# Summing a tile over its partitions: by VectorE and a small matmul, or by TensorE from the whole tile

## The chip, the cores and the metric

The kernel runs on one core of one Trainium2 chip. A core has TensorE (PE in the profile, its weight loads PEld), VectorE (DVE), ScalarE (ACT), GpSimd (POOL) and SyncE (SP, which here only starts DMAs). The metric is device time in microseconds (us); the kernel before took 1765.57 us, the median of 3 runs from 1759.98 to 1765.77.

## The reference, cut to what matters

A token matrix of 256 x 1024 passes through a GLA layer, a grouped mixture of experts (moe0), an mLSTM layer, a second mixture (moe1), and then two transformer layers (l0, l1), each of attention and an MLP. The change touches one small thing in the last two: six rows that scale and shift the activations, made from a vector c that does not depend on the tokens.

```python
c_act = jax.nn.silu(c)                          # 1 x 1024
for l in range(DEPTH):                          # DEPTH = 2
    ada = c_act @ w_ada[l] + b_ada[l]           # (1 x 1024) @ (1024 x 6144)
    sh1, sc1, gt1, sh2, sc2, gt2 = jnp.split(ada, 6, axis=-1)
    h = rms(x, g_mix[l]) * (1.0 + sc1) + sh1    # ahead of attention
    ...
    x = x + gt1 * (mixed @ w_out[l])            # attention's output projection
    h2 = rms(x, g_mlp[l]) * (1.0 + sc2) + sh2   # ahead of the MLP
    x = x + gt2 * (square(relu(h2 @ w_ff1[l])) @ w_ff2[l])
```

## The kernel before, in words

All matrix work is done in float32 precision by three matmuls of a high and a low part: each weight chunk (128 x 1024) is copied to `hi` by ScalarE or VectorE, and `lo = w - hi` is made by VectorE or GpSimd. Dense products accumulate in PSUM tiles `mm` or `acc`. The instructions of every engine stand in the order in which the Python program emits them; the program keeps a clock of its own (class `Clock`, costs in `Timed.cost`) and lets it choose between two engines (`Either`, names `VG`, `VG2`, `AV`), and between emitting a side task's next step or not. Side tasks are generators that `B.tick()` advances between groups of matmuls. The profile puts nearly every instruction on line 175, where the recording wrapper calls the engine, so rows are told apart by tile names.

The modulation `c_act @ w_ada` is such a side task: `ada_cols` (line 1854). A product of a vector with a matrix would use one column of TensorE, so the other engines do it. There are 24 blocks of 512 output columns, numbered n = 0 to 23 (twelve per layer, j = n % 12), each in four quarters q = 0 to 3; a quarter is a DMA of 512 KB into `ada_w` (two buffers, on SP's queue in order with all weight loads), a scaled copy by ScalarE into an `ada_t` tile (128 x 512), a multiply-add of the other half by VectorE, and for q > 0 an add into the block's sum `acc`. There are 96 quarters. A quarter's buffer comes free after its multiply-add, and only then the load of the quarter two further on is issued (line 1904). The three `ada_t` tiles are shared out by `ada_used` (line 1893). In moe1 two free ones also take expert weights (`ada_room`).

After q = 3, `acc` holds 128 partial sums per column, one per partition, and these have to be added over the partitions. Lines 1924 to 1929 do most of it on VectorE: a transposition in blocks of 32 x 32, then a sum over each block's rows, which leaves `part` (128 x 16). Then `reduce` (line 1932), a hook that waits in the list `hooks`, makes four matmuls of 32 output rows against a constant `c_fold` (lines 2441 and 2468). In the trace each float32 matmul is two records, so a reduction shows 8 MATMUL and 8 LDWEIGHTS. Its result is copied to `raw`, the bias is added into `adac`, and for some j the scale and shift columns `mod` are made.

Where a reduction's matmuls stand on TensorE is decided by whoever takes a hook out of the list: the start or the middle of a dense product (lines 580 to 586, 601, 628 to 634), the output projection (line 670), an idle moment of draining (line 512), or `ada_need` (line 1957), which is called where the program cannot go on without a block: it advances side tasks until the block is done, and emits no other matmul meanwhile. In layer l0 that is block 9, needed by the normalization ahead of the MLP (line 2318). Side tasks are also paced: `calm` (line 1950) holds a step back while its engine is behind, and line 1890 holds q = 1 while more than one reduction waits.

Of the kernel before, what the change touches and what calls it, by code (L numbers as in the profile page):

```python
# [26 lines left out]
F32 = mybir.dt.float32  # L27
# [4 lines left out]
OP = mybir.AluOpType  # L32
AX = mybir.AxisListType

P = 128
# [192 lines left out]
def tile_model(ctx: ExitStack, tc: tile.TileContext, I, out, stages=None, h_in=None):  # L228
    nc = tc.nc
    clock = Clock()  # L230
    PE, V, A, G = [Timed(clock, e, n) for e, n in
                   ((nc.tensor, "PE"), (nc.vector, "V"), (nc.scalar, "A"), (nc.gpsimd, "G"))]
# [8 lines left out]
    const = ctx.enter_context(tc.tile_pool(name="const", bufs=1))  # L241
# [163 lines left out]
    def kp_view(W, r0, rows, n0, n):  # L405
        return W[r0:r0 + rows, n0:n0 + n].rearrange("(k p) n -> p k n", p=P)
# [164 lines left out]
    hooks = Hooks()  # L571
# [205 lines left out]
    def gla():  # L777
# [23 lines left out]
        def load_ng(nb):  # L801
            ngs[nb] = bcast_row(ph, I["gla_norm_g"][:, nb * 512:(nb + 1) * 512], "row", 512)
        load_ng(0)
        small_loads()
        glr = early.tile([17, T], F32, name="glr")
        S.pump()
# [177 lines left out]
        if "l0" in stages:  # L984
            B.push(ada_cols(), side=True)
# [859 lines left out]
    ada_T, ada_used = [], {}  # L1845
# [8 lines left out]
    def ada_cols():  # L1854

        todo = [(l, j, q) for l in range(2) if f"l{l}" in stages for j in range(12) for q in range(4)]
        ws = {}

        def load(i):
            if i < len(todo) and i not in ws and not ada_stop:  # L1860
                l, j, q = todo[i]
                ada_open[0] += 1
                w = clock.slot("ada_w", 2, ada.tile([P, 2, 512], F32, name="ada_w", tag="ada_w", bufs=2))
                SP.dma_start(w, kp_view(I["w_ada_2"][l], q * 256, 256, j * 512, 512))
                ws[i] = w

        first = {g: next((i for i, (u, _) in enumerate(S.chunks) if S.units[u][3] == g), 0) for g in ("l0", "l1")}
        NB = (4, 10, 16, 22, 24)
        CB = [first["l0"] - 30, first["l0"] + 36, first["l1"] - 24, first["l1"] + 40, first["l1"] + 90]

        def start(x):
            i = max(j for j in range(4) if x >= NB[j])
            return CB[i] + (CB[i + 1] - CB[i]) * (x - NB[i]) / (NB[i + 1] - NB[i])

        load(0)
        load(1)
        yield 14
        ada_T.extend(ada.tile([P, 512], F32, name="ada_t", tag=tag, bufs=n) for tag, n in
              (("ada_acc", 1), ("ada_t", 2), ("ada_t", 2)))
        acc = None  # L1880
        for i, (l, j, q) in enumerate(todo):
            n = i // 4
            ada_at[0] = lambda: (load(i), load(i + 1))
            while i not in ws:
                load(i)
                load(i + 1)
                yield 6 if i in ws else 1
            while n >= 4 and S.chunk_at < start(n + q / 4):
                yield
            while q == 1 and len(hooks.fs) > 1:  # L1890
                yield
            w = ws[i]
            ada_used[n, q] = (n + (0, 2, 1, 2)[q]) % 3
            t = ada_T[ada_used[n, q]]
            if n >= 4:
                yield from calm("A", w)
            A.activation(t, w[:, 0], AF.Copy, scale=ccol[:, 2 * q:2 * q + 1])
            if n >= 4:
                yield from calm("V", t)
            else:  # L1900
                yield
            V.scalar_tensor_tensor(t, w[:, 1], ccol[:, 2 * q + 1:2 * q + 2], t, op0=OP.mult, op1=OP.add)
            ada_open[0] -= 1
            load(i + 2)
            if q:
                if n >= 4:
                    yield from calm("G", t)
                else:
                    yield 1
                VG2.tensor_tensor(acc, acc, t, op=OP.add)  # L1910
                if q < 3:
                    del ada_used[n, q]
            else:
                acc = t
                if n < 4:
                    yield 1
            if q < 3:
                yield
                continue
            if n >= 4:  # L1920
                yield from calm("V", acc)
            else:
                yield
            part = small.tile([P, 4, 4], F32, name="part", bufs=3)
            V.transpose(t, acc)
            if n >= 4:
                yield from calm("V")
            V.tensor_reduce(part.rearrange("p k r -> p (k r)"), t.rearrange("p (b i) -> p b i", i=32), axis=AX.X,
                            op=OP.add)
            del ada_used[n, 0], ada_used[n, 3]  # L1930

            def reduce(ps, l=l, j=j, part=part):
                for r in range(4):
                    PE.matmul(ps[32 * r:32 * r + 32, 0:4], c_fold, part[:, :, r], start=True, stop=True,
                              skip_group_check=True)
                k = slice(4 * j, 4 * j + 4)
                raw = small.tile([P, 4], F32, name="raw", bufs=2)
                AV.copy(raw, ps[:, 0:4])
                VG2.tensor_tensor(adac[:, l, k], raw, bada[:, l, k], op=OP.add)
                if j % 6 == 3:  # L1940

                    w = j // 6
                    V.tensor_copy(mod[:, l, w, 1], adac[:, l, 24 * w:24 * w + 8])
                    V.scalar_tensor_tensor(mod[:, l, w, 0], adac[:, l, 24 * w + 8:24 * w + 16], 1.0,
                                           gcol[:, l * 2 + w], op0=OP.add, op1=OP.mult)
                ada_done.add((l, j))
            hooks.append(reduce, part)
            yield

    def calm(e, *aps):  # L1950
        for _ in range(10):
            t = max([clock.t[e]] + [clock.last(clock.span(a), False, e) for a in aps])
            if t <= clock.t["PE"] + 0.9:
                return
            yield
# [474 lines left out]
    c_ident = ident  # L2430
# [7 lines left out]
                SP.dma_start(h[a * 64:a * 64 + 64, mt], rows[2 * mt + a])  # L2438
    n_kept = _OFFS[4][0]
    cst = const.tile([P, n_kept - P], F32, name="cst")  # L2440
    c_fold = const.tile([P, 32], F32, name="fold")
    c_ones, c_iota, c_earl = [cst[:, o - P:o - P + n] for o, n in _OFFS[1:4]]
    mhalf = const.tile([P, 16], F32, name="mhalf")
    G.memset(mhalf, -0.5)
# [20 lines left out]

    def small_loads():
        ld = SP.dma_start
        V.tensor_reduce(c_fold, c_ident.rearrange("p (b m) -> p m b", m=32), axis=AX.X, op=OP.add)
        ld(cst, I["cst"][:, P:n_kept])
        ld(rwg[:, 0], I["router_w"].rearrange("(k p) n -> p k n", p=P))  # L2470
        for a, n in enumerate(("ln_g", "ln_b")):
            ld(lnpk[:, a], I[n][:, 0].rearrange("l (p k) -> p l k", k=8))
        ld(gatew, I["mlstm_w_in"][0][:, 4096:4104].rearrange("(k p) n -> p k n", p=P))
        for a in range(2):
            ld(bg[32 * a:32 * a + 4], I["mlstm_b_gates"][0, 4 * a:4 * a + 4].unsqueeze(1))
        ld(crow[0:64], I["mlstm_conv_w"][0].rearrange("j (f p) -> (j f) p", p=P))
        ld(crow[64:80], I["mlstm_conv_b"][0].rearrange("(f p) -> f p", p=P))
        ld(cb16.rearrange("p a b -> p (a b)"), I["cst"][:, _OFFS[4][0]:_OFFS[4][0] + 2 * P])
# [82 lines left out]
    small = ctx.enter_context(sm_cm)  # L2561
# [21 lines left out]
    if first:  # L2583
        with tc.tile_pool(name="ring_b", bufs=RB) as rb, tc.tile_pool(name="rt", bufs=1) as rp, \
# [3 lines left out]
            if "gla" not in stages:  # L2588
                S.pump()
                small_loads()  # L2590
# [6 lines left out]
            for i, s in enumerate(first):  # L2597
                nxt = (first + second)[i + 1] if i + 1 < len(first + second) else None
                with tc.tile_pool(name="ph_" + s, bufs=1) as ph:
# [8 lines left out]
                    else:  # L2608
                        l = int(s[-1])
# [20 lines left out]
    else:  # L2630
        S.pump()
        small_loads()
        for _ in setup():
            pass
        B.push(ada_cols(), side=True)
    if second and not first:
        xin = rms_in(int(second[0][1]), 0)
# [34 lines left out]
```

## Time and profile before

| What | Value |
|---|---|
| median of 3 runs | 1765.57 us |
| lowest and highest run | 1759.98 and 1765.77 us |
| the profiled execution's own time | 1753.21 us |
| its span, first to last instruction | 1751.4 us |
| mean granted clock of TensorE | 0.950 |
| TensorE, VectorE, ScalarE, GpSimd busy | 90%, 63%, 33%, 23% of the span |

All rows below are of the one profiled execution, and times in them count from the span's start. The stages lie roughly so: GLA to 180 us, moe0 to 455, mLSTM to 640, moe1 to 868, attention of l0 to 1110, its MLP to 1310, attention of l1 to 1550, its MLP to the end. TensorE's sums of busy time count the modelled length of each matmul, and following matmuls overlap, so the start of one to the start of the next tells more than the length of one.

### The profile page before, as it was taken

Reading aid. Unit: us, or ns where it says so; the run is one execution under the profiler, and the core shown is the slowest. Engines: PE = TensorE matmul, PEld = TensorE weight load, DVE = VectorE, ACT = ScalarE, POOL = GpSimd, SP = SyncE. Lnnn points to the kernel's source line nnn. Section 1 sums busy time; section 2 is a strip of 40 time slices with the busy share of each in tenths; the row PEclk is TensorE's granted clock in tenths of the full one; section 3 lists DMA queues with packets and bytes.
Section 4 is the critical chain, followed back from the end, with each engine's and each line's share of the span. In section 5 each row is a group of like instructions: output and inputs, shape, how many; then the busy total and the mean of one; then the engine's idle time right before and its main releaser. Section 6 shows DMA issues by size and latency. Waiting matters only on the chain.

```text
span 1751.4 us, 22692 instructions
## 1 busy us (share of the span) xinstructions
PE 1581.4 (90%) x8774; PEld 1139.0 (65%) x8774; DVE 1109.6 (63%) x1730; ACT 574.6 (33%) x973; POOL 396.8 (23%) x266
## 2 busy tenths in 40 slices
PE   7998999898698889989788998889997889989997
PEld 5865434337586544444366797778985678878996
DVE  4776113107786631111478989899887887879875
ACT  5223111115543221111244543534434455342210
POOL 1232000002332200000164324333124541313110
PEclk9998999898899989999889999999998999999999
DMA  9746999999555489999643566578763546546651
GB/s 316 269 146 231 354 399 410 391 348 245 166 181 193 156 306 378 402 408 393 215 155 123 184 200 204 169 258 294 252 229 126 165 129 194 170 154 227 196 183 46
DMA packets 163215, 418.80 MB, mean 239 GB/s; under 512 B 12239, under 2 KB 12907, under 8 KB 152086
## 3 DMA queue, kind: packets, MB, share of 16 engines
q1 hardware_dynamic: 162902, 417.11, 68.3%
q8 instruction: 73, 1.20, 0.3%
q14 instruction: 48, 0.39, 0.1%
q0 software_dynamic: 192, 0.10, 0.0%
HBM read 416.13 MB, written 1.05 MB: 238 GB/s over the span
## 4 chain that ended last, share of the span: by engine, by line
PE 31%; DVE 11%; issue 6%; POOL 3%; ACT 2%; DMA 1%; DVEq 0%; POOLq 0%; ACTq 0%
PE mm L175 16%; PE acc L175 7%; DVE ada_t L175 2%; POOL lo L175 2%; PE up L175 2%; DVE lo L175 1%; PE dn L175 1%; PE sb L175 1%; DMA ada_w<-in_w_ada 1%; DVE xs L175 1%; DVE ro L175 1%; POOL cs L175 1%; DVE h L175 1%; DVE rt L175 1%; ACT pa L175 1%
## 5 line engine op out<-in xcount | busy, mean ns | idle before, releaser
L175 POOL TENSOR_TENSOR lo<-w,hi 128x1024 fp32r<-128x1024 f32 x103 | 262.1, 2550 | 469.5 <-ACT hi L175 415.5
L175 DVE TENSOR_TENSOR lo<-w,hi 128x1024 fp32r<-128x1024 f32 x205 | 262.4, 1285 | 18.9 <-ACT hi L175 13.2
L175 ACT CAST hi<-w 128x1024 fp32r<-128x1024 f32 x207 | 214.8, 1051 | 147.6 <-PE mm L175 100.6
L175 PE MATMUL mm<-hi,X_H 128*128 128x512 f32 x512 | 222.4, 434 | 27.5 <-ACT X_H L175 14.4
L175 PE MATMUL mm<-lo,X_H 128*128 128x512 f32 x512 | 213.7, 417 | 15.9 <-POOL lo L175 13.2
L175 PE MATMUL mm<-X_H,hi 128*128 128x256 f32 x704 | 204.2, 290 | 0.5 <-DVE raw L175 0.5
L175 PE MATMUL mm<-hi,X_L 128*128 128x512 f32 x512 | 199.5, 413 | 4.4 <-DVE X_L L175 4.4
L175 PE MATMUL mm<-X_L,hi 128*128 128x256 f32 x704 | 200.0, 284 | 0.0
L175 PE MATMUL mm<-X_H,lo 128*128 128x256 f32 x704 | 199.9, 284 | 0.0
L175 PE MATMUL up<-w,X 128*64 128x512 f32 x672 | 193.9, 598 | 0.7 <-ACT X L175 0.7
L175 PEld LDWEIGHTS mm<-hi,X_H 128*128 128x128 f32 x512 | 103.8, 203 | 60.0 <-issue 17.9
L175 PEld LDWEIGHTS mm<-X_H,hi 128*128 128x128 f32 x704 | 135.3, 192 | 2.7 <-DVE raw L175 0.9
L175 PEld LDWEIGHTS mm<-X_L,hi 128*128 128x128 f32 x704 | 135.5, 192 | 0.4
L175 PEld LDWEIGHTS mm<-X_H,lo 128*128 128x128 f32 x704 | 135.4, 192 | 0.0
L175 PEld LDWEIGHTS mm<-lo,X_H 128*128 128x128 f32 x512 | 103.8, 203 | 38.6 <-POOL lo L175 14.4
L175 DVE SCALAR_TENSOR_TENSOR y<-dn,gsl,y 128x512 fp32r<-128x512 f32 x32 | 24.0, 751 | 161.9 <-ACT y L175 161.9
L175 PEld LDWEIGHTS mm<-hi,X_L 128*128 128x128 f32 x512 | 102.1, 200 | 31.1 <-DVE X_L L175 7.8
L175 PEld LDWEIGHTS up<-w,X 128*64 128x64 f32 x672 | 58.6, 137 | 96.8 <-issue 93.0
L175 PE MATMUL up<-wh,X 128*64 128x512 f32 x336 | 115.0, 596 | 0.0
L175 PE MATMUL dn<-w,hTt 128*64 128x512 f32 x336 | 105.5, 632 | 2.1 <-ACT hTt L175 2.1
L175 PE MATMUL acc<-lo,fh 128*128 128x512 f32 x256 | 100.5, 392 | 0.5 <-DVE lo L175 0.5
L175 PE MATMUL acc<-hi,fl 128*128 128x512 f32 x256 | 100.8, 394 | 0.0
(416 smaller groups left out, 2774.7 us busy)
## 6 DMA issues: line engine op xcount, KB each, us to landing
w<-in_moe_w SPq DMA_DIRECT2D x126, 1024.0 KB
w<-in_w_ff SPq DMA_DIRECT2D x64, 1024.0 KB
wh<-in_moe_w SPq DMA_DIRECT2D x124, 512.0 KB
ada_w<-in_w_ada SPq DMA_DIRECT2D x96, 512.0 KB
w<-in_w_in SPq DMA_DIRECT2D x40, 1024.0 KB
w<-in_mlstm_w_in SPq DMA_DIRECT2D x16, 1024.0 KB
w<-in_gla_w_in SPq DMA_DIRECT2D x12, 1024.0 KB
w<-in_w_out SPq DMA_DIRECT2D x8, 1024.0 KB
```

The costliest lines, as they stand in the source:

```text
L175: r = f(*args, **kw)
```

## The change: what it does

The transposition, the sum over rows, the tile `part` and the constant `c_fold` go. `reduce` now takes the whole tile: four matmuls, each with 128 columns of `acc` as weights (128 x 128) and one column of ones as the moving operand, so that each gives 128 sums, already one per partition. The tile that holds `acc` now stays taken until the reduction has been emitted, not only until VectorE has read it. So the tiles are shared out in another way, and the wait of line 1890 is replaced: q = 2 of block n takes the tile that held the sum of block n - 1, and waits until that block's reduction has left the list.

```diff
-            while q == 1 and len(hooks.fs) > 1:
+            while (n - 1, 0) in ada_used and q == 2:
                 yield
             w = ws[i]
-            ada_used[n, q] = (n + (0, 2, 1, 2)[q]) % 3
+            ada_used[n, q] = (n + (0, 1, 2, 1)[q]) % 3
             t = ada_T[ada_used[n, q]]
...
-            part = small.tile([P, 4, 4], F32, name="part", bufs=3)
-            V.transpose(t, acc)
-            if n >= 4:
-                yield from calm("V")
-            V.tensor_reduce(part.rearrange("p k r -> p (k r)"), t.rearrange("p (b i) -> p b i", i=32), axis=AX.X,
-                            op=OP.add)
-            del ada_used[n, 0], ada_used[n, 3]
-
-            def reduce(ps, l=l, j=j, part=part):
-                for r in range(4):
-                    PE.matmul(ps[32 * r:32 * r + 32, 0:4], c_fold, part[:, :, r], start=True, stop=True,
+            del ada_used[n, 3]
+
+            def reduce(ps, l=l, j=j, n=n, acc=acc):
+                for f in range(4):
+                    PE.matmul(ps[:, f:f + 1], acc[:, f * P:(f + 1) * P], c_ones[:, 0:1], start=True, stop=True,
                               skip_group_check=True)
+                del ada_used[n, 0]
...
-            hooks.append(reduce, part)
+            hooks.append(reduce, acc)
...
-    c_fold = const.tile([P, 32], F32, name="fold")
...
-        V.tensor_reduce(c_fold, c_ident.rearrange("p (b m) -> p m b", m=32), axis=AX.X, op=OP.add)
```

Engine by engine the rest of the program keeps its instructions: TensorE has as many as before, VectorE 49 fewer in these sums and 7 `lo` more, GpSimd 7 `lo` fewer. But side work changes its place. The largest shift is in l0, at the end of the attention's output projection. The first place is VectorE there: `res` and `h` are the residual of one half row block (the first two pairs of a block of 128 tokens, mt = 0, then of mt = 1), `ada_t` the quarters, `adac` and `mod` the result of block 9. Before:

```order
L175 SCALAR_TENSOR_TENSOR ada_t<-ada_w,ccol,ada_t 128x512
L175 TENSOR_TENSOR lo<-w,hi 128x1024
L175 TENSOR_TENSOR ada_t<-ada_t 128x512
L175 STREAM_TRANSPOSE ada_t<-ada_t 128x512
L175 TENSOR_REDUCE part<-ada_t 128x16
L175 SCALAR_TENSOR_TENSOR ada_t<-ada_w,ccol,ada_t 128x512
L175 TENSOR_TENSOR adac<-raw,bada 128x4
L175 COPY mod<-adac 128x8
L175 SCALAR_TENSOR_TENSOR mod<-adac,gcol 128x8
L175 TENSOR_TENSOR lo<-w,hi 128x1024
L175 TENSOR_TENSOR res<-mm,gt 128x512
L175 TENSOR_TENSOR h<-h,res 128x512
```

and with the change, from the second residual on:

```order
L175 TENSOR_TENSOR res<-mm,gt 128x512
L175 TENSOR_TENSOR h<-h,res 128x512
L175 SCALAR_TENSOR_TENSOR ada_t<-ada_w,ccol,ada_t 128x512
L175 TENSOR_TENSOR ada_t<-ada_t 128x512
L175 SCALAR_TENSOR_TENSOR ada_t<-ada_w,ccol,ada_t 128x512
L175 TENSOR_TENSOR ada_t<-ada_t 128x512
L175 SCALAR_TENSOR_TENSOR ada_t<-ada_w,ccol,ada_t 128x512
L175 TENSOR_TENSOR ada_t<-ada_t 128x512
L175 TENSOR_TENSOR adac<-raw,bada 128x4
L175 COPY mod<-adac 128x8
L175 SCALAR_TENSOR_TENSOR mod<-adac,gcol 128x8
L175 TENSOR_TENSOR rs<-ss 128x1
```

Block 9's last quarter (number 39) and its `mod` stood ahead of the first residual; now the quarters 37, 38 and 39 stand behind the second. On TensorE the block's four matmuls stand, in the new order, behind the matmuls of mt = 0 and ahead of all 24 of mt = 1.

The second place is SP's queue over the same time: `w` from `w_out` and `w_ff` are weight loads, `ada_w` the quarters. Before:

```order
L175 DMA w<-in_w_out 128x4x512
L175 DMA ada_w<-in_w_ada 128x2x512
L175 DMA w<-in_w_ff_2 128x4x512 x2
L175 DMA ada_w<-in_w_ada 128x2x512
L175 DMA w<-in_w_ff_2 128x4x512
L175 DMA ada_w<-in_w_ada 128x2x512
L175 DMA w<-in_w_ff_2 128x4x512
L175 DMA ada_w<-in_w_ada 128x2x512
L175 DMA w<-in_w_ff_2 128x2x1024
```

and with the change:

```order
L175 DMA w<-in_w_out 128x4x512
L175 DMA ada_w<-in_w_ada 128x2x512
L175 DMA w<-in_w_ff_2 128x4x512 x2
L175 DMA ada_w<-in_w_ada 128x2x512
L175 DMA w<-in_w_ff_2 128x4x512
L175 DMA ada_w<-in_w_ada 128x2x512
L175 DMA w<-in_w_ff_2 128x4x512
L175 DMA ada_w<-in_w_ada 128x2x512 x6
L175 DMA w<-in_w_ff_2 128x2x1024 x2
```

Before the first `w_ff` load 41 quarters had been issued, now 36; the quarters 38 to 43 come in one row, each behind the multiply-add of the quarter two before it, and the MLP's first two down-projection loads stand behind them.

## Rows read from the trace of the kernel before

**Rows 1.** The page: busy us and share by engine; then groups, busy, mean ns.
```profile
PE 1581.4 (90%) x8774; PEld 1139.0 (65%) x8774; DVE 1109.6 (63%) x1730; ACT 574.6 (33%) x973; POOL 396.8 (23%) x266
...
L175 POOL TENSOR_TENSOR lo<-w,hi 128x1024 fp32r<-128x1024 f32 x103 | 262.1, 2550 | 469.5 <-ACT hi L175 415.5
L175 DVE TENSOR_TENSOR lo<-w,hi 128x1024 fp32r<-128x1024 f32 x205 | 262.4, 1285 | 18.9 <-ACT hi L175 13.2
```

**Rows 2.** Stretches: us, PE, PEld, DVE, ACT, POOL busy; clock, DMA share, GB/s.
```profile
640.00:868.00 228.00, 211.09 (x1006) 91.55 (x1006) 43.20 (x76) 38.08 (x62) 9.36 (x7) 0.97 0.93 361
868.00:1086.00 218.00, 192.08 (x1203) 160.85 (x1203) 183.77 (x307) 101.36 (x202) 87.86 (x65) 0.93 0.55 176
1120.00:1230.00 110.00, 102.31 (x664) 91.92 (x663) 102.57 (x113) 50.70 (x71) 37.54 (x14) 0.97 0.75 256
1230.00:1310.00 80.00, 79.74 (x501) 70.92 (x500) 69.12 (x81) 30.99 (x41) 15.87 (x7) 1.00 0.74 255
1310.00:1480.00 170.00, 146.65 (x845) 120.29 (x844) 142.93 (x256) 78.09 (x167) 70.17 (x55) 0.92 0.49 155
```

**Rows 3.** By tile, `ada_t`: count, ns least, median, greatest; first and last start.
```profile
L175 ACT ACTIVATE ada_t<-ada_w,ccol x96: 705/723/766, 51.9 to 1628.4; 128x512 f32<-128x512 f32 x96
L175 DVE SCALAR_TENSOR_TENSOR ada_t<-ada_w,ccol,ada_t x96: 737/747/2901, 69.6 to 1637.6; 128x512 f32<-128x512 f32 x96
L175 DVE TENSOR_TENSOR ada_t<-ada_t x63: 675/692/2901, 73.3 to 1638.3; 128x512 f32<-128x512 f32 x63
L175 DVE STREAM_TRANSPOSE ada_t<-ada_t x24: 697/711/714, 100.7 to 1639.1; 128x512 f32<-128x512 f32 x24
L175 DVE TENSOR_REDUCE part<-ada_t x24: 676/686/689, 101.5 to 1639.8; 128x16 f32<-128x512 f32 x24
```

**Rows 4.** Groups by form: busy us, mean ns; idle before, what ended it.
```profile
L175 PE MATMUL mm<-part,fold 128*32 128x4 f32 x128 | 4.0, 186 | 4.4 <-DVE part L175 4.4
L175 PE MATMUL bgp<-part,fold 128*32 128x4 f32 x56 | 1.7, 181 | 5.1 <-DVE part L175 5.1
```

**Rows 5.** TensorE in order of time: start, us, what; `adar`, then a reduction.
```profile
1013.12 0.28 PE L175 MATMUL mm<-X_H,lo 128*128 128x256 f32 x1
1013.24 1.05 PE L175 MATMUL adar<-ident,adac 128*128 128x128 f32 x8
1014.05 0.36 PE L175 MATMUL mm<-X_H,hi 128*128 128x256 f32 x1
...
1059.88 0.28 PE L175 MATMUL mm<-oaTh,lo 128*128 128x256 f32 x1
1060.08 0.25 PE L175 MATMUL mm<-part,fold 128*32 128x4 f32 x8
1060.26 0.38 PE L175 MATMUL mm<-oaTh,hi 128*128 128x256 f32 x1
```

**Rows 6.** TensorE's waits, 868 to 1086, then 1310 to 1480: us, times, longest.
```profile
PE pta L175 <- DVE pa L175: 3.2, 2, 3.0
PE mm L175 <- DVE th L175: 1.8, 1, 1.8
...
PE mm L175 <- DVE xs L175: 3.4, 1, 3.4
PE tpd L175 <- DVE diag L175: 2.1, 1, 2.1
```

**Rows 7.** Around l0's output projection, in order of time; then two chain pieces.
```profile
1097.44 0.68 DVE L175 TENSOR_TENSOR res<-mm,gt 128x512 f32<-128x512 f32 x1
1098.16 0.69 DVE L175 TENSOR_TENSOR h<-h,res 128x512 f32<-128x512 f32 x1
...
1109.77 0.80 PE L175 MATMUL mm<-hi,X_H 128*128 128x512 f32 x1 [5.95 <-ACT X_H L175]
...
1158.18 6.74 DMA ada_w<-in_w_ada
1188.47 4.76 DMA ada_w<-in_w_ada
```

## The prediction

> **What bounds the kernel now.** I read the page's busy shares first. TensorE has 90%, VectorE 63% [rows 1]. That is a mean over unlike stages, so the stretches come next [rows 2]: in moe1 the DMA share is 0.93 and VectorE has 43 of 228 us to do; in l0's attention VectorE is busy 183.77 of 218 us and TensorE 192.08; in the first part of l0's MLP 102.57 and 102.31 of 110; from 1230 to 1310 TensorE is busy 79.74 of 80; l1's attention looks like l0's, 142.93 and 146.65 of 170. The reader is to see two engines that take turns, neither far from full. Time taken off VectorE comes back only where TensorE waits for it, and time added to TensorE costs wherever it does not already wait. The waits say where that is [rows 6]: in l0's attention up to 1086 TensorE waited for VectorE 12.4 us (five entries of the view, 3.2, 3.1, 2.3, 2.0 and 1.8, first and last shown), in l1's 10.9 us (four entries, 3.4, 2.7, 2.7, 2.1). For the sums themselves it waited 4.4 and 5.1 us, 9.5 in all, in four reductions [rows 4].
>
> **The change part by part.** *TensorE's groups get longer.* From the last matmul ahead of a reduction to the first behind it are 0.38 us; two such neighbours are 0.12 apart, so the group costs 0.26 [rows 5]. The new group is not in this trace. It has as many records, but with weights of 128 columns where `fold` has 32. The nearest is `adar`, which has 8 records with 128-column weights and 128 moving columns: 0.93 from neighbour to neighbour, so 0.81 [rows 5]. With one moving column it can be shorter, but each record still loads its own weights, so I take 0.81, with 0.26 as the lower end (one moving column as cheap as the old group) and 1.05, the length of the whole `adar` group, as the upper. That adds 0.55 us to each of 24 groups, 13.2 in all (0 to 19). Three of the old groups stood directly ahead of a wait of 1.8 us or more, which takes the addition up. The four early ones (before 868 us) come ahead of MoE stages that run at the DMA's rate; I let half of these count. So 24 - 3 - 2 = 19 groups, **+10.5 us**.
>
> *VectorE loses the transposition and the sum over rows*: 0.711 + 0.686 = 1.40 us for each of 24 blocks, 33.5 us [rows 3]. The sum over `ident` for `c_fold` goes too; it is one short instruction at the very start, under the first loads, and I cost it at nothing. What comes back: the four reductions that TensorE waited for have their data 1.40 earlier, 5.6 us (at most the 9.5 of rows 4). In the two attentions, 12.4 + 10.9 us of waits hang on a queue that loses five and three such pairs, 11.2 us; since the queue is busy 84% of the time [rows 2], but only part of it is ahead of what TensorE waits for, I take half, 5.6. A further 0.7 for the one block at the start of l1's MLP whose transposition is on the chain. Together **-11.9 us**; the ends are 0 (all of it in slack) and the whole 33.5.
>
> *Work moves.* Up to the start of `w_ff`'s loads five quarters fewer are issued than before. So up to 1086 VectorE has five multiply-adds and adds fewer to do, 5 x (0.747 + 0.692) = 7.2 us [rows 3]. TensorE's waits at the end of the attention that this can shorten are the last entries, 1.8 and 2.0; I take **-2** (0 to -4).
>
> The price is behind it. In the new order TensorE stands at block 9's reduction ahead of all 24 matmuls of mt = 1, and cannot pass it. Ahead of it on VectorE stand the second residual and quarters 37, 38 and 39. The second residual was read at 1097.44 and its `h` done at 1098.16 + 0.69 = 1098.85 [rows 7]. Quarter 37's multiply-add ends 0.75 later, at 1099.6. Only then is its buffer free for quarter 39's load; such a load took 4.76 us on the chain where it came alone [rows 7], so 1104.4; then ScalarE 0.72, the multiply-add 0.75, the add 0.69 [rows 3], 1106.5, and the group 0.81, 1107.3. Before, TensorE had gone on at about 1097.4, so it is 9.9 us late. It did wait later, 5.95 us for `X_H` ahead of the MLP [rows 7]; I let 3.4 of that absorb, since the residual, its squares and the scaling still follow the last matmul. Remains **+6.5 us**. Queued behind the waiting reduction are the matmuls of mt = 1 and the MLP's first products; the `w_ff` loads of the down projection, now behind quarter 43 on SP, are not used until some 15 us into the MLP, and I cost their delay at nothing; if that cover were gone it would be one load, 4 to 7 us. The lower end is 0, if load 39 finds the way free earlier because VectorE is ahead; the upper end takes 6.74 us for a load [rows 7], for quarter 39 and again for quarter 41, whose multiply-add now stands ahead of mt = 1's residual: about +10.3.
>
> *Seven splits `lo` go from GpSimd to VectorE*: 7 x 1.285 = 9.0 us more on the one, 7 x 2.55 = 17.9 less on the other [rows 1]. A split is done sooner on VectorE and what follows on it comes later; I take 0, between -6 and +6. Here a row calls for a second reading: the multiply-adds have a median of 747 ns and a greatest of 2901, the adds 692 and 2901, while the transpositions end at 714 and the sums at 689 [rows 3]. So the removed instructions never were the stretched ones, and the stretching stays unless GpSimd runs less. The Trainium skill ("SBUF — State Buffer", section "SBUF: two separate sides") states that VectorE and GpSimd hold a shared pair of ports as an exclusive lock for a whole instruction, and that an instruction of VectorE with two SBUF inputs needs it against a GpSimd instruction that reads SBUF. The trace agrees as to which rows are stretched. By that rule removing the pairs frees no lock and seven fewer splits free seven; without it the stretch would be chance and stay. What this would make of the time is a rival below.
>
> *The sum*: 10.5 - 11.9 - 2 + 6.5 + 0 = +3.1 us, on the profiled execution 1753.2 + 3.1 = 1756.3. That execution is 12.4 us under the median of the runs, 1765.57; the difference between two kernels does not depend on it, so I forecast 1765.6 + 3.1 = **1768.7 us**. A measurement of this kernel can tell about 0.5%, 8.8 us, from no change, so this is the same time.
>
> **The rivals.** *VectorE was the real bound.* Then the 17 blocks between 868 and 1590 us give back their whole 1.40, 23.7 us, the longer groups cost 10.5, and the block 9 stall is met by the lead that VectorE has gained: -13.2, about 1752. For it: VectorE above 84% in both attentions and 93% in the first part of the MLP [rows 2]. Against it: TensorE's own share there is as high.
>
> *The stall at block 9 decides.* Loads of 6.74 us make it +10.3, and VectorE's relief reaches TensorE only in the four reductions that waited: 10.5 - 5.6 + 10.3 = +15.2, about 1781. For it: an order in which SP, ScalarE, VectorE and TensorE each wait for one another, and the waits for `ada_w` on the chain. Against it: TensorE already waited 5.95 us at this place. It counts as slower once the stall, less what the wait absorbs, exceeds about 12 us with the rest as I have it.
>
> *The lock.* A multiply-add beside a GpSimd split takes up to 2.901 - 0.747 = 2.15 us longer [rows 3]. Seven splits fewer would save VectorE 7 x 2.15 = 15 us, 6 more than the 9.0 it takes over. If all of that reached the path the time would be 1768.7 - 6 = 1762.7.
>
> **How the numbers follow.** The forecast has 0.38, the bound on VectorE 0.24, the stall 0.27, the lock 0.11. The first and the last lie within 8.8 us of 1765.6: same 0.49, faster 0.24, slower 0.27. The likeliest case's own range, from the bounds of its terms, is 1758 to 1778. For 8 in 10 the range has to reach into both other cases: 1751 to 1784.
>
> **What would show it right or wrong.** In the changed kernel's profile the reduction's group should take about 0.9 us from neighbour to neighbour; if it takes under 0.5, the first term is gone. VectorE's busy time should fall by about 33.5 - 9.0 - 3 x 0.69 = 22 us. TensorE should show a wait for an `ada_t` of VectorE or GpSimd at block 9's reduction, near 1100 us, of 5 to 12 us, and the MLP of l0 should start 3 to 8 us later than it did. The waits for `part` should come back as waits for `ada_t`, each over 1 us shorter. The prediction fails if l0's attention ends earlier than before, or if more than 10 us appear or vanish in a stage where I count nothing, moe0, mLSTM or moe1.

## The result, and the profile after

The changed kernel took 1784.51 us, the median of 4 runs from 1780.88 to 1788.57, against 1763.24 us for 4 runs of the kernel before: a ratio of 1.0129, 95% interval 1.0103 to 1.0155, or 18 to 27 us slower. (The ratio is not simply that of the two medians, 1.0121, which lies inside its interval; so it is with every ratio below.) The forecast was 1768.7 us, no change, in a range up to 1784. Below, ratios are turned into microseconds with 1760 us, and "before" is always run on the same chip as what it is compared with. The difference between two such ratios, as between the change and one of the runs below, is known only to about 5 or 6 us.

The profiled execution of the changed kernel has a span of 1786.8 us. Its page, answering to [rows 1]: busy us and share by engine, then the two groups of splits.

```profile
PE 1609.0 (90%) x8772; PEld 1168.6 (65%) x8774; DVE 1094.0 (61%) x1690; ACT 574.1 (32%) x971; POOL 383.1 (21%) x259
...
L175 POOL TENSOR_TENSOR lo<-w,hi 128x1024 fp32r<-128x1024 f32 x96 | 242.7, 2535 | 502.2 <-ACT hi L175 447.2
L175 DVE TENSOR_TENSOR lo<-w,hi 128x1024 fp32r<-128x1024 f32 x212 | 271.6, 1286 | 22.9 <-ACT hi L175 17.4
```

VectorE and GpSimd have less to do than before, TensorE has 28 us more, by modelled lengths, and the program is longer. The new group itself, in order of time, beside the second half of [rows 5]:

```profile
1021.89 0.28 PE L175 MATMUL mm<-X_H,lo 128*128 128x256 f32 x1
1022.01 0.95 PE L175 MATMUL mm<-cst,ada_t 128*128 128x1 f32 x8
1022.82 0.36 PE L175 MATMUL mm<-X_H,hi 128*128 128x256 f32 x1
```

From neighbour to neighbour it is 0.93 us, where the old group took 0.38: the 0.55 longer that the prediction took from `adar`. Paid in full, that is 13 us over 24 groups, not the 23 of the result. The rest has to be in what TensorE waits for. The groups by form, answering to [rows 4] (busy us, mean ns; idle before, what ended it):

```profile
L175 PE MATMUL mm<-cst,ada_t 128*128 128x1 f32 x120 | 15.2, 247 | 1.6 <-DVE ada_t L175 1.6
L175 PE MATMUL bgp<-cst,ada_t 128*128 128x1 f32 x64 | 11.0, 293 | 23.1 <-DVE ada_t L175 19.4 <-DVE mixed L175 3.7
```

The sums were waited for by 9.5 us before, and by 24.7 now; 3.7 of these, in mLSTM, are for something that VectorE's `mixed` released and not for the sum's data. Most of the rest is in l0. TensorE's waits from 1086 to 1300 us (who waited for whom, us in total, times, longest), the kernel before first:

```profile
PE mm L175 <- ACT X_H L175: 6.0, 1, 6.0
PE mm L175 <- DVE part L175: 4.4, 1, 4.4
PE bgp L175 <- DVE part L175: 3.3, 2, 2.0
```

and with the change:

```profile
PE bgp L175 <- DVE ada_t L175: 19.4, 3, 9.3
PE mm L175 <- ACT X_H L175: 2.1, 1, 2.1
PE mm L175 <- DVE lo L175: 2.0, 4, 1.2
```

The sums, for which TensorE waited 7.7 us here, now cost 19.4. The longest is block 9's, ahead of the second half of l0's output projection. The chain that ends in it, in order of time (start, us, what), answers to [rows 7]:

```profile
1107.06 0.70 DVE res L175
...
1108.40 0.76 DVE ada_t L175
...
1109.17 4.75 DMA ada_w<-in_w_ada
...
1114.01 0.73 ACT ada_t L175
...
1114.76 0.76 DVE ada_t L175
...
1115.55 0.70 DVE ada_t L175
...
1116.30 1.87 PE bgp L175 x8
```

TensorE's own row for that group, with its wait in brackets:

```profile
1116.30 1.87 PE L175 MATMUL bgp<-cst,ada_t 128*128 128x1 f32 x8 [9.27 <-DVE ada_t L175]
```

This is the chain of the prediction, link by link: second residual, quarter 37's multiply-add, the load of quarter 39 which had to wait for it, scaled copy, multiply-add, add, group. What the working had too small is the last line. The group takes 1.87 us there, twice its usual length. The stretches around it show why (us, then busy us by engine, then the granted clock, DMA share, GB/s): the matmuls ahead of the wait, the group and what follows, and the end of it.

```profile
1104.00:1107.00 3.00, 3.00 (x14) 2.15 (x12) 2.96 (x4) 0.59 (x2) 0.00 (x0) 1.00 0.47 115
1116.30:1120.00 3.70, 3.70 (x13) 3.31 (x14) 1.34 (x6) 0.79 (x2) 0.90 (x1) 0.50 0.57 180
1120.00:1123.00 3.00, 3.00 (x9) 2.32 (x8) 1.04 (x2) 1.76 (x2) 1.05 (x2) 0.50 0.62 177
1123.20:1126.00 2.80, 2.80 (x14) 2.31 (x13) 2.25 (x3) 0.72 (x2) 1.50 (x2) 1.00 0.59 179
```

After standing for 9.27 us TensorE was granted 0.50, its 1.2 GHz level, until about 1123 us; from there it had 2.4 GHz again. Matmuls of 512 columns followed each other every 0.43 us in place of 0.23. So this wait cost its 9.27 us, 0.92 for the slow group, and twelve matmuls at 0.2 more, 2.4: some 12.6 us.

The stretches of [rows 2], with the change (us, PE, PEld, DVE, ACT, POOL busy; clock, DMA share, GB/s):

```profile
640.00:868.00 228.00, 218.06 (x1038) 92.78 (x1034) 35.95 (x64) 37.72 (x57) 3.13 (x4) 0.98 0.96 372
868.00:1086.00 218.00, 189.53 (x1189) 161.31 (x1190) 174.88 (x302) 97.95 (x201) 81.76 (x62) 0.93 0.53 168
1120.00:1230.00 110.00, 101.42 (x599) 90.54 (x597) 90.77 (x98) 51.28 (x79) 38.54 (x17) 0.94 0.63 211
1230.00:1310.00 80.00, 71.53 (x431) 64.64 (x432) 63.19 (x68) 29.73 (x38) 15.81 (x6) 0.94 0.73 247
1310.00:1480.00 170.00, 147.96 (x783) 121.83 (x781) 141.56 (x244) 74.66 (x155) 71.65 (x55) 0.92 0.49 159
```

From 1230 to 1310 TensorE had been busy 79.74 of 80 us at clock 1.00; now it is 71.53 at 0.94, with 431 matmuls where there were 501. VectorE is less busy there too. (By 1230 us the changed kernel is some 23 us behind, so its window holds earlier work.) Neither engine is full; both wait. Followed matmul by matmul, the two profiled executions stand 10 us apart at 1088 us, 20 at the start of l0's MLP, 35 at 1250, and 34 to 38 from there to the end. (That is more than the 23 of the medians, since the profiled execution of before was a short one and this one a long one.) About 9 to 12 us arise in mLSTM, 10 at block 9 and 15 in l0's MLP, and nothing in l1. Not all of this is the change's. The profiles of E1, E2, E3 and E11 below, all in the order of before or near it, fall 3 to 10 us behind the same profile of before in l0's MLP, so that execution was a fast one there. The loss in mLSTM is firmer: from 455 to 640 us all six profiles with the change's order there (the change, E4, E5, E6, E9, E10) fall 6 to 13 us behind, the others 0 to 5.

### The profile page after: what moved, and what is told of

Read it like the earlier page. It is cut to its first block, busy times and chain, and to the rows that moved or that the text cites. A ratio compares the mean times of both kernels' runs of the same rounds, so it can differ in the third digit from the quotient of the medians.

```text
span 1786.8 us, 22631 instructions
## 1 busy us (share of the span) xinstructions
PE 1609.0 (90%) x8772; PEld 1168.6 (65%) x8774; DVE 1094.0 (61%) x1690; ACT 574.1 (32%) x971; POOL 383.1 (21%) x259
## 4 chain that ended last, share of the span: by engine, by line
PE 32%; DVE 11%; issue 5%; POOL 3%; DMA 2%; ACT 2%; DVEq 0%; POOLq 0%; ACTq 0%; SPq 0%
PE mm L175 18%; PE acc L175 6%; DMA ada_w<-in_w_ada 2%; DVE ada_t L175 2%; PE up L175 2%; DVE lo L175 1%; PE dn L175 1%; PE sb L175 1%; POOL cs L175 1%; DVE xs L175 1%; POOL lo L175 1%; ACT pa L175 1%; DVE rt L175 1%; DVE ro L175 1%; DVE h L175 1%
## 5 line engine op out<-in xcount | busy, mean ns | idle before, releaser
L175 POOL TENSOR_TENSOR lo<-w,hi 128x1024 fp32r<-128x1024 f32 x96 | 242.7, 2535 | 502.2 <-ACT hi L175 447.2
L175 DVE TENSOR_TENSOR lo<-w,hi 128x1024 fp32r<-128x1024 f32 x212 | 271.6, 1286 | 22.9 <-ACT hi L175 17.4
L175 PE MATMUL up<-wh,X 128*64 128x512 f32 x320 | 108.5, 601 | 0.0
L175 DVE SCALAR_TENSOR_TENSOR ada_t<-ada_w,ccol,ada_t 128x512 f32<-128x512 f32 x96 | 92.7, 966 | 23.0 <-ACT ada_t L175 20.3
```

What stands on the lines that cost most here:

```text
L175: r = f(*args, **kw)
```

## The experiments

The question was which part is slow: the operations (longer groups, less VectorE work), or the order in which they now stand. The program's clock lets them be parted: it adds up what each instruction should cost, and the order follows from it. An instruction can be emitted without being charged to that clock, and another charged without being emitted, so that every engine keeps one kernel's order while the operations are the other's.

**E1, long groups alone.**

```diff
-                    PE.matmul(ps[32 * r:32 * r + 32, 0:4], c_fold, part[:, :, r], ...)
+                    PE.eng.matmul(ps[:, 4 * r:4 * r + 4], c_ident, part[:, :, r], ...)
+                    # the old matmul is charged to the program's clock
```

> The kernel before, with its own order on every engine, but the four matmuls of each of the 24 sums take a 128 x 128 constant as weights in place of the 128 x 32 one (the sums are then not the reference's). Only the length of the groups on TensorE changes, from 0.38 to about 0.93 us from neighbour to neighbour. Theory A (the longer groups are paid in full wherever TensorE does not already wait): 24 x 0.55 = 13.2 us, 10 to 15 more than before, about 1775. Theory B (the groups lie beside weight loads or ahead of waits and cost little; the order of work made the change slow): 0 to 5 more.

Measured: 1.0033, interval 1.0016 to 1.0051, that is +5.8 us (3 to 9). That is about half of theory A's 13 and near theory B's upper end of 5. The other half presumably falls into time that TensorE would have waited anyway; which groups that were is not shown.

**E2, VectorE's pair away alone.**

```diff
-            V.transpose(t, acc)
-            V.tensor_reduce(part..., t..., axis=AX.X, op=OP.add)
+            V.eng.tensor_copy(part[...], acc[:, 0:16])
+            # both old instructions are charged to the program's clock
```

> The kernel before, with its own order on every engine, but VectorE's transposition and sum over rows are replaced by one copy of 16 columns (the sums are then not the reference's): some 24 x 1.3 = 31 us less work on VectorE. Theory A, as forecast (relief comes back in the four sums that were waited for and in half of the attentions' pairs): 12 us less than before, about 1751. Theory B (the relief falls into slack, except where TensorE waited for the sums): 3 to 6 less. Theory C (VectorE was the bound): 24 less.

Measured: 0.9963 (0.9944 to 0.9982), -6.5 us (3 to 10 less): just past theory B's upper end, and half of theory A's relief, which the interval leaves out. The edit took less away than expected, since the copy that stands in for the pair is not always short (count, ns least, median, greatest):

```profile
L1929 DVE COPY part<-ada_t x24: 161/175/2376, 101.1 to 1639.2; 128x16 f32<-128x16 f32 x24
```

Six of the 24 copies took 0.66 to 2.38 us, and all together 14.3. So VectorE lost 19 us of the pair's 33.5 and not 31, and 6.5 is not the price of the whole pair.

**E3, both edits.**

> Both edits of the two runs beside it at once, in the order of the kernel before: what the change would cost if it moved nothing (sums not the reference's). If the order made the change slow: within 5 us of before or faster (13 - 12 = +1 as forecast). If the operations themselves made it slow: most of the +21 us of the change shows here, 1778 or more.

Measured: 1.0015 (0.9997 to 1.0033), +2.6 us (none to 6). The copies take 14.6 us here, so this is the price with part of VectorE's relief still missing. In the order of the kernel before, the change's operations would have cost next to nothing.

**E4, the order alone.**

```diff
-            del ada_used[n, 3]
+            V.eng.transpose(t, acc)
+            V.eng.tensor_reduce(part..., t..., axis=AX.X, op=OP.add)
+            del ada_used[n, 3]
...
+                    PE.eng.matmul(ps[32 * r:32 * r + 32, 0:4], c_fold, part[:, :, r], ...)
+                    # the new matmul is charged, not emitted
```

> The changed kernel's order on every engine, with the operations of the kernel before: VectorE's transposition and sum over rows, and groups with 128 x 32 weights. Only the order, and with it the place of the loads, differs from before. If the order made the change slow: 15 to 25 us more than before, about 1780 to 1788. If the longer groups did, and the order only moves the stall at block 9 by the forecast 6.5 us less the 2 gained: about 4 more, 1768.

Measured: 1792.54 us, 1.0167 (1.0141 to 1.0193), +29 us (25 to 34), more than the 15 to 25 expected. The old operations in the new order are slower than the change itself. TensorE's waits from 1086 to 1300 us in that run (its `part` is written on a line of its own):

```profile
PE bgp L1932 <- DVE part L1926: 30.9, 4, 10.4
PE mm L1932 <- DVE part L1926: 3.5, 1, 3.5
PE mm L175 <- ACT X_H L175: 2.7, 1, 2.7
```

34.4 us for the sums, where the same operations in the old order waited 7.7. Together with E3 this shows that the order makes the change slow. It does not yet show what in the order does.

**E9, short groups in the new order.** Weights of 32 columns of `acc` and four moving columns of ones, all else as changed.

> The changed kernel in its own order, each of the 24 groups with 128 x 32 weights instead of 128 x 128 (sums of a quarter of the columns only, not the reference's). If the longer groups cost here what the same edit added to the kernel before (+0.33%): 6 us less than the changed kernel, 1778. If they cost more because they stand behind waits at the slow clock: 10 to 13 less, 1773. If the waits swallow them: 0 to 3 less.

Measured: 1.0093 (1.0069 to 1.0117), +16.4 us over before, 6.3 less than the change. With E4 this prices the two operations in the new order: the longer groups 6.3 us, as in the old one (5.8), and the removed pair 29.4 - 16.4 = 13 us. Each of the two differences is uncertain by about 6 us, so the first does not decide between the three theories. That the second is twice E2's 6.5 does not show that the relief counts more in the new order, since E2 took away 19 us and this is the whole pair, 33.5.

**E5 and E6, the loads of the late quarters.**

```diff
-                SP.dma_start(w, kp_view(I["w_ada_2"][l], q * 256, 256, j * 512, 512))
+                if not (i // 4 in (9,) and q > 1):      # E6: (9, 11, 15)
+                    SP.dma_start(w, kp_view(I["w_ada_2"][l], q * 256, 256, j * 512, 512))
```

> The changed kernel, its order kept, without the loads of block 9's third and fourth quarter (they take the data of its first two; the sums of that block are then not the reference's). Theory A (TensorE's 9.3 us ahead of block 9's sum are the chain residual, multiply-add, load, copy, multiply-add, add, of which the load is 4.75): the wait falls to about 4.5 us and the time by 5 to 7 us, to 1778, the slow clock after it included. Theory B (the residual and VectorE's queue make the wait, the load lies beside them): 0 to 1 us less.

> As the run beside it, and the same for blocks 11 and 15, whose sums TensorE waits for by 4.6 and 5.6 us in l0's MLP (these sums are not the reference's either). Theory A (all three waits hang on loads of quarters that are issued late): 12 to 18 us less than the changed kernel, about 1769. Theory B (l0's MLP is bound by VectorE's queue and the waits come back elsewhere in it): not more than 3 us beyond the run beside it.

Measured: 1.0120 (1.0100 to 1.0140) and 1.0113 (1.0093 to 1.0132), so 1.6 and 2.8 us less than the change, less than the intervals can tell apart (about 6). Theory A falls in E6, which was to gain 12 to 18; in E5 its 5 to 7 are not excluded. In both profiles block 9's wait did shrink, from 9.27 us to 5.77 and 5.78, by 3.5 of the load's 4.75. In E5's, block 8's group ahead of it, which had not waited in the profile of the change, waited as well:

```profile
1099.48 1.87 PE L175 MATMUL bgp<-cst,ada_t 128*128 128x1 f32 x8 [5.76 <-DVE ada_t L175]
1113.58 1.87 PE L175 MATMUL bgp<-cst,ada_t 128*128 128x1 f32 x8 [5.77 <-DVE ada_t L175]
```

The edit need not have made that wait: E6's profile, with the same edit at block 9, has none there. TensorE came to block 8's group at 1093.7 us in E5 and at 1101.8 with the change, where 3.4 us of waits for `X_H` and `X_L` and then a granted clock of 0.50 lay ahead of it (E5: 0.7 us for `X_L`); VectorE's add for it ended at about the same time in both, 1099.4 and 1099.6.

In E6, blocks 11 and 15 still waited, 4.18 and 5.62 us (with the change 4.55 and 5.59), without a load of their own last quarters to wait for. Block 15's group with the change, then in E6:

```profile
1265.62 1.84 PE L175 MATMUL bgp<-cst,ada_t 128*128 128x1 f32 x8 [5.59 <-DVE ada_t L175]
1259.00 1.84 PE L175 MATMUL bgp<-cst,ada_t 128*128 128x1 f32 x8 [5.62 <-DVE ada_t L175]
```

What stood ahead of block 15's last add is VectorE's own queue, here with GpSimd's row first:

```profile
1249.36 5.64 POOL L175 TENSOR_TENSOR lo<-w,hi 128x1024 fp32r<-128x1024 f32 x2 [2.93 <-ACT hi L175]
```

```profile
1249.82 2.37 DVE L175 TENSOR_TENSOR adac<-raw,bada 128x4 f32<-128x4 f32 x1
1252.11 0.68 DVE L175 CAST hi<-w 128x1024 fp32r<-128x1024 f32 x1
1252.82 3.26 DVE L175 TENSOR_TENSOR lo<-w,hi 128x1024 fp32r<-128x1024 f32 x1
1256.01 0.74 DVE L175 SCALAR_TENSOR_TENSOR ada_t<-ada_w,ccol,ada_t 128x512 f32<-128x512 f32 x1
```

An add of four columns, usually 0.15 us, takes 2.37, and a split of 1.23 takes 3.26; each ends within about a microsecond of one of GpSimd's two splits (1252.17 and 1255.00 us). Block 15's late quarter did not wait for its load, but for what was in front of it on VectorE. At block 9 the load was one link of several: without it, 5.8 of 9.3 us stayed.

**E7, blocks 0 to 3 as before.**

```diff
-            while (n - 1, 0) in ada_used and q == 2:
+            while len(hooks.fs) > 1 and q == 1 if n < 4 else (n - 1, 0) in ada_used and q == 2:
                 yield
...
+            if n < 4:   # transposition, sum over rows, c_fold, and the tile given back at once
```

> The changed kernel, but blocks 0 to 3 (GLA and mLSTM) are summed and paced as in the kernel before, so that all is in the old order up to moe1's end, and two more quarters are loaded before l0's MLP (38, not 36). Theory A (the new order costs some 9 us in mLSTM, and block 9 stands later for every quarter that was not loaded): 10 to 15 us less than the changed kernel, about 1772. Theory B (the 9 us in mLSTM are chance of one profile): 0 to 4 less.

Measured: 1771.00 us, 1.0056 (1.0037 to 1.0074), 13 us less than the change, about 6 either way: theory A. In its profile block 9 still waits 3.87 us, block 11 4.55 and block 15 5.62.

**E8, the sum taken when its data is ready.** As E7, and:

```diff
             while ... (n - 1, 0) in ada_used and q == 2:
+                if n > 4 and hooks:
+                    if bgtag[0] == "acc":
+                        yield from room(1)
+                    if hooks:
+                        hooks.pop(0)(bg_ps())
                 yield
```

> As the run beside it, and a block that waits for the tile of the block before it now has that block's sum made at once, between two groups of matmuls, as soon as its data is there by the program's clock; 42 quarters are loaded before l0's MLP (before: 41). Theory A (the held tile made the quarters late, and that made the change slow): block 9's wait is gone, and the time is that of the kernel before plus the longer groups less VectorE's relief, 1758 to 1766, no slower than before. Theory B (the longer hold or the sums in the middle of a product cost by themselves): 1772 or more.

Measured: 1758.74 us, 0.9995 (0.9980 to 1.0009): no slower than before, all of the loss is gone. Block 9's group now stands ahead of the output projection, at 1074.84 us, and waits 0.33 us; the waits for sums from 1086 to 1300 us are 6.9 us:

```profile
PE mm L175 <- DVE ada_t L175: 6.9, 2, 5.0
PE mm L175 <- ACT X_H L175: 6.0, 1, 6.0
```

**E10, the same without restoring mLSTM.**

> The changed kernel with its new paths and order up to moe1's end (mLSTM not restored), but with the sums made as soon as their data is there from block 5 on, as in the run that was the same as before; 38 quarters are loaded before l0's MLP. If mLSTM and l0 are two separate costs of the order, 9 and 11 us: 10 to 12 less than the changed kernel, 1773. If block 9 needs the two quarters that mLSTM's order held back as well: 0 to 6 less.

Measured: 1759.85 us, 1.0002 (0.9987 to 1.0017): 22 us less than the change, about twice what I expected. So taking the sums when they are ready repairs all of it alone, and E7's 13 us and this do not add up. Its profile still shows the 9 us lost in mLSTM, and a wait of 3.70 us at block 9, but none of note at blocks 11 and 15; it stands 3.8 us ahead of before at 125 us, and loses less than E8 in l0's MLP, 4.4 us against the profile of before from 1086 to 1286 where E8 loses 9.5. Why that part runs better with 38 quarters loaded than with 42 stays open. So does how much of mLSTM's 9 us is in the 23.

**E11, the same in the kernel before.**

> The kernel before, its transposition and sum on VectorE and its short groups kept, with sums made as soon as their data is there from block 5 on, in place of holding a block while two wait; 42 quarters are loaded before l0's MLP. If early taking only repairs the held tile: the same as before, within 4 us. If it is worth something by itself, 5 or more less than before, then the run of the changed kernel with it hid a cost of the change of that size.

Measured: 0.9991 (0.9976 to 1.0007), the same as before. By itself early taking is worth nothing that these runs can tell (4 us less to 1 more); it repairs what the held tile did.

**E12, block 0 from the whole tile too.** E8's `n < 4` becomes `0 < n < 4`.

> The kernel of the run with sums taken when ready and the old mLSTM, with block 0 (in GLA) summed from the whole tile as well, so that VectorE's pair is gone there too; all else in the same order. The profiles of kernels without that pair in GLA stand 2.4 to 3.8 us ahead of the kernel before at 160 us. If that lead is kept to the end: 3 us less than with the pair, 1755 to 1756, 0.2 to 0.3% faster than before. If moe0, which runs at the rate of its loads, takes it back: the same as before, within 2 us.

Measured: 1753.13 us, 0.9953 (0.9939 to 0.9968): 8 us faster than before and 31 faster than the change, the best of all. The gain over E8, about 7 us by the ratios, is more than the lead in its profile accounts for (3 us at 120 us, and two waits in GLA, 1.0 us for `eb` and 1.2 for `X_L`, that before and E8 have and it has not). Where the rest comes from is not shown.

## Why the prediction was wrong

**Which step failed: "Work moves".** The prediction summed the new order as -2 for five quarters fewer and +6.5 for one stall. The order alone costs 29 us (E4). The step treated the five late quarters as work saved for VectorE up to 1086 us, and counted one place where that is paid back. They are paid back at later sums whose place on TensorE is fixed by the program: at block 9 (9.27 us), then at 11 (4.55) and 15 (5.59) in l0's MLP, where the prediction even booked a gain for the sums that were waited for; and mLSTM, where the step counted nothing, loses another 9 to 12. That the cause is the held tile, with sums that wait for a fixed place, is shown by E8, E10 and E11: with the sums taken early the loss is gone, and early taking alone gains nothing. How the 29 us divide over mLSTM, block 9 and the MLP stays open, since E7 and E10 do not add up.

**The stall at block 9 was the right mechanism, at too small a price.** TensorE was to be 9.9 us late with a group of 0.81, a wait of 9.1; it was 9.27. Of what follows, 3.85 us were absorbed ahead of the MLP (the wait for `X_H` fell from 5.95 us to 2.1; I had 3.4). The size was off mainly by what TensorE's clock did after it, +0.92 in the group and 2.4 in the matmuls, and the offset between the profiles grew by 10.3 us from 1088 us to the MLP instead of 6.5. (Of these, 0.5 is block 8's longer group, which the prediction booked elsewhere.) That it is also the +10.3 of the rival "the stall decides" is luck: the load took 4.75 us, not 6.74 (and twice 1.98 on 6.5 makes +10.5). That rival's time, 1781, was the nearest of all, but by its own condition, a stall that leaves over 12 us, it did not come in; the loss was spread over three places. I gave it 0.27, because I let TensorE's later wait speak against it.

**The longer groups.** 0.55 us each was exact, +10.5 in all too much: 5.8 and 6.3 (E1, E9). That more of them fell ahead of waits than the five that I took off is likely and not shown.

**VectorE's relief.** -11.9 was forecast for the whole pair. With 19 of its 33.5 us away the old order gave -6.5 (E2), with all of it the new one -13, give or take 6 (E9 against E4); so this term is not refuted. The sums that were waited for did not come earlier by 1.40 us each: in E2's profile the waits at three of them fell by 0.8 to 1.0, but two that stood behind a copy of 2.2 us were waited for by 2.1 and 0.8 us more, and all together it is 10.0 us, where it was 9.5. What the two attentions gave back there is some 3 us of waits for VectorE, not 5.6. In sum, the operations were forecast at -1.4 and measured at +2.6 (E3). That they agree is partly luck: the longer groups were put about twice too high, and E3's relief was short of the whole pair's.

**The rivals.** "VectorE was the real bound" is out: it had 23.7 us for the whole pair, by rough proportion (an estimate) some 13 for the 19 of 33.5 us that E2 took away, and E2 gave 6.5 (3 to 10). "The lock" is out as a gain: counted over the whole profile, 62 instructions of VectorE took 1.5 to 2.4 us longer than the median of the same instruction on the same tiles before the change, and 65 after it; with seven fewer GpSimd splits there were not fewer of them. No run changed these splits alone. But its rows were worth more than the rival made of them, since such stretched instructions stood ahead of block 15's sum, with the change as in E6.

**The marks that were named.** The group takes 0.93 us: as said. VectorE's busy time fell by 15.6 us, not 22, mainly since the multiply-adds and the small adds became longer: the mean of the first went from 908 to 966 ns, and 22 adds into `adac` took 10.2 us, where 20 had taken 3.2. The wait at block 9 came as said, 9.27 us. The MLP of l0 was to start 3 to 8 us later than it did; it started 20.2 later (1129.95 for 1109.77). The waits for `part` came back as waits for `ada_t`, longer and not shorter. A loss of more than 10 us in a stage where nothing was counted was named as a sign of failure, and it came about so in mLSTM (9 to 12).

## What to carry to other kernels

When a change lets an intermediate tile live longer, ask first who can no longer start because of it, and follow that work to the next place where the program's order makes an engine stand for it; the cost of the operations that are exchanged may be the small part. In a program whose order is chosen by a cost model, part the two by freezing one kernel's order under the other's operations, before explaining either. And where a result is consumed at a fixed place, take it when it is ready instead: that turned 23 us of loss into none, and with the first block too into a gain of 8.

## What the runs showed of the hardware

Waits of TensorE cost more than themselves here: after the 9.27 us at block 9 the granted clock was 0.50 for 6.8 us, and in mLSTM after 3.68 us it was 0.50 for 6.8 as well. A wait of 2.06 us ahead of l0's MLP, with the change, was followed by a clock of 0.51 from 1129.95 to 1133.40 us. The stretches in mLSTM:

```profile
533.00:535.60 2.60, 2.60 (x12) 1.88 (x10) 1.55 (x10) 0.00 (x0) 0.82 (x2) 1.00 0.38 158
539.40:545.80 6.40, 6.40 (x19) 5.43 (x20) 5.22 (x10) 2.77 (x5) 0.24 (x2) 0.50 0.40 97
546.40:552.00 5.60, 5.60 (x27) 4.62 (x26) 4.50 (x5) 1.83 (x4) 1.14 (x1) 1.00 1.00 399
```

These are the stretches ahead of that wait, from the group on, and after. The group took 1.82 us instead of 0.95, and twelve matmuls 5.2 us from the first start to the one behind the last, where twelve at 0.23 take 2.7: 3.4 us for a wait of 3.7. The sum over partitions from the whole tile, four matmuls of one moving column, took 0.81 us in all, as long as the same number of records with 128 moving columns (`adar`, [rows 5]): what counts in these rows is the weights' 128 columns, not the moving ones. E1's groups, with 128 columns of weights and four moving ones, take 0.93 from neighbour to neighbour too, and E9's, with 32 and four, 0.38. Very short instructions of VectorE can be stretched as far as long ones: an add of 128 x 4, usually 0.15 us, took 2.37 beside a GpSimd split (E6), a copy of 128 x 16, usually 0.17, up to 2.38 (E2).
